# The passage from the output projection to the up projection in a decoder layer: weights in places of their own, operands made within the last output block, and a written order

## The chip, the cores and the metric

The kernel is one program on one core of a Trainium2 chip. A core has a matrix engine (TensorE, PE in the profile; its weight loads are listed apart as PEld), VectorE (DVE), ScalarE (ACT), GpSimd (POOL) and SyncE (SP), on whose queue this kernel issues all its DMAs. Each engine works through its own instructions in order and waits on semaphores for the others. The metric is the time of one execution in microseconds on the device.

## The reference

One layer on x of 2048 x 1024, in float32. The mixer's three head groups yield y, which is projected and added; then comes a gated, convolved feed-forward network with 2816 channels a half. What lies around the change:

```python
y = jnp.concatenate([y_attn, y_mlstm, y_sgu], axis=-1)
x = x + gt1 * (y @ w_out)                        # output projection
h = rms_norm(x, g_ffn) * (1.0 + sc2) + sh2       # 2048 x 1024
z = h @ w_up                                     # up projection, to 2 x 2816
z = causal_depthwise_conv(z, w_conv, b_conv)     # width 3
a, gv = jnp.split(z, 2, axis=-1)
x = x + gt2 * ((silu(a) * gv) @ w_down)
```

## The kernel before

**Precision.** A float32 operand is split into a high and a low half in fp32r, and a product is three matmuls: high by high, high by low, low by high (`mm3`, lines 54 to 56). Making the halves costs a cast on ScalarE (the high half) and a subtraction of two SBUF operands on another engine (the low half), mostly VectorE.

**The output projection** works on four blocks of 512 positions, `TBS = (2, 3, 0, 1)`. A block has eight parts (i, nb), 128 positions by 512 columns; a part is 24 matmuls of 128x512 into a bank of PSUM (`wps`), with operands `yhl0`/`yhl1` (the split y, loaded on SP as `yt_d` and, for half of them, `y2_d`, which are added on VectorE) and `wo0`/`wo1` (the split w_out). Loads pass through three buffers `ld`. A part is evicted on VectorE (`evict`: times gate, plus x, then squares on ScalarE). When both halves of a row tile are done, `stats` works out the scale of the norm (its last operation on GpSimd) and `scale` applies it on VectorE. When all four row tiles of a block are scaled, `turns` transposes them: eight tiles k, each of four 128x128 transposes on TensorE into a bank `tps` (four banks), then a copy on ScalarE to `hT[k]`, which is called hz in the trace. `turns` of a block stands within the parts of the next one, behind its part 1. Blocks 0 and 1 (positions 1024 to 2047, H = 1) are also made into operands of the up projection by `put_d` and written to memory as `hc_d` for later.

**The up projection** uses a product scheme with seven instead of eight block products. A group g is 128 columns of each half of w_up; H is the half of the positions. Its seven steps p = 1, 2, 5, 6, 7, 4, 3 take the operands B11, B21, T1, T2, T3, T4, B22, four tiles each of 512 columns, made once for each H from hT. B11 and B21 need only the first 512 positions of a half, thus the third output block; T1 = B12 - B11, T3 = B22 - B12, T2 = B22 - T1, T4 = B21 - T2 and B22 need the last one. The weights' side of a step is a quarter of the group's tiles w1, w2 or a combination of them, S1 or S2; `Group.prep` makes it and splits it (the tiles wsph and wspl), three steps ahead. `Group.mm` issues 12 matmuls, `Group.post` combines the results, and `conv` and `gate` follow as VectorE and ScalarE have time. The first two groups of H = 0 run interleaved: steps 0 and 1 are both groups' p = 1, steps 2 and 3 both groups' p = 2, then p = 5, and so on to step 13. Group 2 begins at step 14.

**What sets the order.** The instructions are written in an order by Python code, and a scheduler then reorders them on each engine by its own costs. In this kernel it interleaved the passage: one T1 matmul stands ahead of the steps on B21, and the combinations T1, T3, T2 and T4 alternate with S1, S2 on VectorE. Memory on the core is given out by pools that open and close like a stack on a left and a right side; a tile waits until the former user of its place is done. The weights `w` of the first two groups lie where `wo0` was, B11 where `yhl1` was, so both are made only when the output projection ends. `w_first`, the loads of these weights, are written behind the last output block.

The names and lines that matter: `load_split` (loads at 296 and 299, the addition at 300, casts at 130, low half at 131), `put` (1141 to 1154), `evict` (1182, rows L1186 and L1187), `stats` (1192), `scale` (L1200), `turn` (transposes L1208, copy L1209), `turns` (1213), `b_first`, `prep` (S1 and S2 at L1317 and L1318, casts L1327, low halves L1328), the step loop at the end, and `conv` (L1382, L1383, L1387).

Of the kernel before, what the change touches and what calls it, by code (L numbers as in the profile page):

```python
# [8 lines left out]
F32 = mybir.dt.float32  # L9
# [3 lines left out]
ALU = mybir.AluOpType  # L13
# [4 lines left out]
P = 128  # L18
# [15 lines left out]
def trunk(  # L34
# [278 lines left out]
    def up_open_right():  # L313
        pool.open("up_r1", "right", *[("act%d" % n, 4096, 1) for n in range(14, 22)], ("wsp", 2048, 12))
        pool.open("up_r2", "right", ("w", 4096, 4), ("B11", 4096, 4), ("B21", 4096, 4), ("T2", 4096, 4))

# [803 lines left out]

    pool.open("zy", "left", ("zy", 4104, 8))
    pool.open("wo_l", "left", ("hl", 4096, 4), ("gt1", 4096, 1), ("yg", 2048, 2), ("x2", 4096, 6), ("wst_", 8, 8))
# [17 lines left out]

    def put(n, q, t, by_dram=False):

        if n == "T2":
            src = t[:, 1, :].bitcast(F32) if by_dram else pool.tile([P, 512], F32, name="t2")
            V.tensor_tensor(src, h_part("B22", q), h_part("T1", q), op=ALU.subtract)
            V.tensor_tensor(h_part("T4", q), h_part("B21", q), src, op=ALU.subtract)
        else:
            src = h_part(n, q)
            if n == "T1":
                V.tensor_tensor(src, h_part("B12", q), h_part("B11", q), op=ALU.subtract)  # L1150
            elif n == "T3":
                V.tensor_tensor(src, h_part("B22", q), h_part("B12", q), op=ALU.subtract)
        A.copy(t[:, 0, :], src)
        V.tensor_tensor(t[:, 1, :], src, t[:, 0, :].bitcast(F32), op=ALU.subtract)

    def put_d(n, q):
        t = pool.tile([P, 2, 512], F32R, name="hl", tag="hl")
        put(n, q, t, True)
        dma(hc_d[COMBO.index(n), q], t.bitcast(F32))

    class Block:
# [50 lines left out]

        def turns(self):
            if self.half == 0:
                for k in range(KT):
                    self.turn(k)
                if self.H == 1:
                    for q in range(4):
                        todo.append(lambda q=q: (put_d("B11", q), put_d("B21", q)))
            else:  # L1220
                for q in range(4):
                    self.turn(q)
                    self.turn(4 + q)
                    if self.H == 1:
                        todo.append(lambda q=q: (put_d("T1", q), put_d("T3", q)))
                        todo.append(lambda q=q: (put_d("T2", q), put_d("T4", q), put_d("B22", q)))
# [4 lines left out]
    for n, tb in enumerate(TBS):  # L1231
# [3 lines left out]
        for j, (i, nb) in enumerate(parts):  # L1235
# [5 lines left out]
            if prev:  # L1241
                prev[0].evict(*prev[1:])
                if prev[2] == 1:
                    prev[0].stats(prev[1])
                    prev[0].scale(prev[1])
            if j == 1 and before:
                before.turns()
            if todo and j >= 1:
# [5 lines left out]
    while todo:  # L1254
        todo.pop(0)()
    pool.close("wo_r2")
    pool.close("wo_r")
    pool.close("att_s")
    pp.close("wo_r")
    up_open_right()  # L1260
    w_first = [w_load(0), w_load(1)]
    hb = {}

    def b_first(n, qs=range(4)):
        for q in qs:
            t = b_tile(n, q)
            hb.setdefault((0, n), []).append(t)
            put(n, q, t)

    blk.evict(0, 1)  # L1270
    b_first("B11", (0, 1))
    blk.stats(0)
    blk.scale(0)
    blk.evict(1, 1)
    b_first("B11", (2, 3))
    blk.stats(1)
    blk.scale(1)

# [9 lines left out]
    def up_open_left():  # L1288
        pool.open(
            "up_l", "left", ("s", 2048, 4), ("sw", 2048, 4), ("T1", 4096, 4), ("B22", 4096, 4), ("t2", 2048, 1), ("hal", 352, 1)  # L1290
        )
        pp.open("up_l", "left", ("ub1", 2048, 4))
# [4 lines left out]
    class Group:  # L1297
# [12 lines left out]
        def prep(self, p):  # L1310
# [4 lines left out]
            if p in (5, 6) and self.S1 is None:  # L1315
                self.S1, self.S2 = self.tmp("S1", "sw"), self.tmp("S2", "sw")
                V.tensor_tensor(self.S1, A_[2, 1], A_[2, 2], op=ALU.add)  # L1317
                V.tensor_tensor(self.S2, self.S1, A_[1, 1], op=ALU.subtract)  # L1318
            if p == 7:
# [30 lines left out]
        def post(self, p):  # L1350
            g, H = self.g, self.H
            if p == 1:
                self.s1 = self.tmp("s1", "s")
                A.copy(self.s1, self.X)
# [258 lines left out]
    for i in range(AHEAD):  # L1613
        up_groups(-1)
    prep(0)
    blk.evict(2, 1)
    blk.stats(2)
    prep(1)
    blk.scale(2, True)
    blk.evict(3, 1)  # L1620
    b_first("B21", (0, 1))
    blk.stats(3)
    b_first("B21", (2,))
    blk.scale(3, True)
    b_first("B21", (3,))
    prep(2)
    loaded = n_open + 1
    for i, s in enumerate(steps):
# [15 lines left out]
        if i == 1:  # L1644
            blk.turns()
            pool.close("wo_l")
            pp.close("wo_l")
            up_open_left()
            hal = pool.tile([P, 44, 2], F32, name="hal")
            V.memset(hal, 0.0)  # L1650
        if i >= n_open:
            while loaded < min(i + AHEAD + 3, n_left + AHEAD + 3 if i < n_left else len(steps)):
                load(loaded)
                loaded += 1
# [7 lines left out]
        if i:  # L1662
            q = steps[i - 1]
            if q[0] == "up":
                if q[1:] in ((0, 0, 2), (0, 1, 2)):
# [49 lines left out]
```

## Time and profile before

| | us |
|---|---|
| median of 3 runs | 2640.88 (2638.76 to 2641.74) |
| the profiled execution | 2639.6 |
| its span, first to last instruction | 2637.8 |
| mean granted TensorE clock | 0.994 of full speed |
| output projection, about | 1160 to 1349 |
| passage, about | 1349 to 1391 |
| up projection of the first groups | from 1391 |

The profile is of one execution. A row of the timeline gives the start, the duration, the engine, the line, the operation, the tiles it writes and reads, and in square brackets how long the engine was idle before it and what ended the wait. A window's row gives each engine's busy time in a stretch. Where engines are busy in the large stages can be seen in these windows (length; busy us and instructions of PE, PEld, DVE, ACT, POOL; granted clock; DMA share; GB/s), the second one from the passage on:

```text
1160.00:1350.00 190.00, 186.07 (x869) 153.00 (x868) 111.68 (x193) 74.25 (x150) 14.88 (x19) 1.00 0.66 228
1350.00:1440.00 90.00, 80.96 (x342) 64.98 (x341) 85.12 (x130) 54.51 (x100) 0.84 (x1) 0.94 0.28 85
1440.00:2000.00 560.00, 558.81 (x2465) 462.35 (x2464) 471.61 (x622) 268.98 (x449) 0.00 (x0) 1.00 0.33 110
```

### The profile page before, as it was taken

The page shows a single profiled execution, that of the slowest core. Times are in us where ns is not written, and L with a number is a line of the kernel's source. Part 1 is how long each engine was busy: PE and PEld are TensorE (multiplying, and loading weights), DVE is VectorE, ACT ScalarE, POOL GpSimd, SP SyncE. Part 2 cuts the span into 40 slices and gives each one's busy share as a digit, 9 for nine tenths or more (in the row PEclk, how much of TensorE's full clock was granted, in tenths as well). Part 3 has the DMA queues.
Part 4 walks back from the last instruction along what each step waited for, and adds up shares of the span by engine and source line. Part 5 has one row for each costly group of instructions (what it writes and reads, how often), then busy time and mean ns, then how long its engine had stood idle before and what let it go on. Part 6 is the DMA issues. An engine that isn't in the chain of part 4 may idle for free.

```text
span 2637.8 us, 36872 instructions
## 1 busy us (share of the span) xinstructions
PE 2559.2 (97%) x12761; PEld 2116.1 (80%) x12761; DVE 1994.9 (76%) x3454; ACT 1269.7 (48%) x2420; POOL 398.4 (15%) x530
## 2 busy tenths in 40 slices
PE   5999999999999999999989999999999999999999
PEld 4887888878787878777868888888888888888787
DVE  7477644565468888966769888887888888898797
ACT  4333334333367888853455454444444444444443
POOL 2012210122335665630000000000000000000000
PEclk9999999999999999999999999999999999999999
DMA  7554553324563345346723222236222226648523
GB/s 250 183 162 132 178 161 109 105 80 116 160 188 109 113 136 146 87 148 238 276 80 101 83 88 80 86 141 237 88 85 84 80 72 248 235 164 299 182 98 116
DMA packets 297986, 377.51 MB, mean 143 GB/s; under 512 B 31422, under 2 KB 189980, under 8 KB 295752
## 3 DMA queue, kind: packets, MB, share of 16 engines
q1 hardware_dynamic: 297800, 375.16, 44.4%
q8 instruction: 101, 1.65, 0.2%
q14 instruction: 85, 0.70, 0.1%
HBM read 274.34 MB, written 100.74 MB: 142 GB/s over the span
## 4 chain that ended last, share of the span: by engine, by line
PE 78%; DVE 9%; DMA 6%; issue 3%; ACT 2%; POOL 1%; SPq 1%; DVEq 0%; ACTq 0%; POOLq 0%
PE ub L56 10%; PE ub L55 10%; PE ub L54 10%; PE acc L54 6%; PE acc L56 6%; PE acc L55 6%; PE db L55 4%; PE db L56 4%; PE db L54 4%; PE sp L205 3%; PE tp L258 3%; PE op L244 2%; PE op L245 2%; DVE wspl L1459 1%; DMA wa<-in_w_ada_dram 1%
## 5 line engine op out<-in xcount | busy, mean ns | idle before, releaser
L54 PE MATMUL acc<-wh,hh 128*128 128x512 f32 (+2 forms) x768 | 287.6, 376 | 3.3 <-DVE ev L684 1.4
L54 PE MATMUL ub<-T,wsph 128*128 128x512 f32 x704 | 274.4, 390 | 5.8 <-ACT wsph L1327 5.8
L56 PE MATMUL acc<-wh,hl 128*128 128x512 f32 (+2 forms) x768 | 274.9, 361 | 1.9 <-DVE hl L562 1.9
L55 PE MATMUL acc<-wl,hh 128*128 128x512 f32 (+2 forms) x768 | 274.5, 359 | 0.0
L56 PE MATMUL ub<-T,wspl 128*128 128x512 f32 x704 | 273.9, 390 | 0.3 <-DVE wspl L1328 0.3
L55 PE MATMUL ub<-T,wsph 128*128 128x512 f32 x704 | 274.1, 389 | 0.0
L55 PE MATMUL db<-wspl,wsph 128*128 128x512 f32 x616 | 240.6, 391 | 2.8 <-DVE wspl L1459 2.7
L56 PE MATMUL db<-wsph,wspl 128*128 128x512 f32 x616 | 239.8, 390 | 0.0
L54 PE MATMUL db<-wsph 128*128 128x512 f32 x616 | 238.4, 390 | 0.3 <-ACT wsph L1458 0.3
L1327 ACT CAST wsph<-S 128x512 fp32r<-128x512 f32 x176 | 109.6, 623 | 228.7 <-PE ub L55 161.0
L262 DVE TENSOR_TENSOR plo<-tp,phi 128x512 fp32r<-128x512 f32 (+1 forms) x320 | 187.0, 607 | 31.5 <-ACT phi L261 29.2
L54 PE MATMUL ub<-B,wsph 128*128 128x512 f32 x528 | 207.4, 393 | 2.8 <-ACT wsph L1327 2.8
L56 PE MATMUL ub<-B,wspl 128*128 128x512 f32 x528 | 207.3, 393 | 0.8 <-DVE wspl L1328 0.8
L55 PE MATMUL ub<-B,wsph 128*128 128x512 f32 x528 | 207.3, 393 | 0.0
L222 ACT ACTIVATE L<-L,nm 128x1024 f32<-128x1024 f32 (+2 forms) x192 | 172.5, 902 | 36.4 <-DVE nm L211 35.1
L258 PE MATMUL tp<-ident,L 128*128 128x128 f32 x1088 | 177.1, 275 | 2.8 <-DVE plo L262 0.8
L261 ACT CAST phi<-tp 128x512 fp32r<-128x512 f32 (+1 forms) x320 | 159.8, 520 | 40.1 <-PE tp L258 38.8
L205 PE MATMUL sp<-kk,q 128*128 128x512 f32 (+3 forms) x640 | 169.4, 376 | 3.2 <-DVE nm L211 2.2
L227 POOL TENSOR_SCALAR L<-L,rs 128x1024 f32<-128x1024 f32 (+2 forms) x192 | 167.2, 881 | 11.0
L1458 ACT CAST wsph<-act 128x512 fp32r<-128x512 f32 x132 | 82.2, 623 | 179.1 <-PE db L55 162.7
L54 PEld LDWEIGHTS acc<-wh,hh 128*128 128x128 f32 x768 | 146.9, 192 | 23.1 <-DVE ev L684 1.6
L56 PEld LDWEIGHTS acc<-wh,hl 128*128 128x128 f32 x768 | 145.4, 190 | 24.2 <-DVE hl L562 2.7
(337 smaller groups left out, 5998.4 us busy)
## 6 DMA issues: line engine op xcount, KB each, us to landing
w<-in_w_up_dram SPq DMA_DIRECT2D x88, 512.0 KB
wd<-in_w_down_dram SPq DMA_DIRECT2D x176, 256.0 KB
wa<-in_w_ada_dram SPq DMA_DIRECT2D x96, 256.0 KB
act_d<-yc SPq DMA_DIRECT2D x44, 512.0 KB
act<-act_d SPq DMA_DIRECT2D x44, 512.0 KB
wr<-in_w_in_dram SPq DMA_DIRECT2D x64, 256.0 KB
q<-q_d SPq DMA_DIRECT2D x128, 128.0 KB
hc_d<-hl SPq DMA_DIRECT2D x28, 512.0 KB
```

The source lines that it names most:

```text
L54: T.matmul(ps, lh, rh, start=start, stop=False, skip_group_check=resume)
L55: T.matmul(ps, lh, rl, start=False, stop=False, skip_group_check=resume)
L56: T.matmul(ps, ll, rh, start=False, stop=stop, skip_group_check=resume)
L205: T.matmul(sp[:, b : b + bw], q2[n][:, qs], kk[:, s0 + b : s0 + b + bw], start=n == 0, stop=n == 1 and not last)
L222: A.activation(L[c], L[c], AF.Exp, bias=nm[:, n - 1 : n], scale=-1.0, accum_out=rs[:, c : c + 1])
L227: G.tensor_scalar(t, t, rs[:, 0:1], 1.0, op0=ALU.mult, op1=ALU.mult)
L244: T.matmul(op[:, c0:], vv[:, j, :], hi[:, c0:], start=(j == 0), stop=False)
L258: T.transpose(tp[:, i * P : (i + 1) * P], rows[i][j // 8][:, (j % 8) * P : (j % 8 + 1) * P], ident)
L261: A.copy(hi[:, c0:], tp[:, c0:])
L262: V.tensor_tensor(lo[:, c0:], tp[:, c0:], hi[:, c0:].bitcast(F32), op=ALU.subtract)
L1327: A.copy(hi, src)
L1458: A.copy(hi, v)
```

## The change

It has five parts. (1) The weights of the first two groups get places of their own: the tag `w` moves into the pool `zy` on the left, opened with the output projection; B11 and B21 move to where `wo0` and `yhl1` were, and s1 of the first two groups gets a tag `s0` of its own. The loads are written at part 0 of the last output block. (2) `turns` is split into two parts of four tiles, behind part 1 and part 2 of the next block. (3) B11 and the weights' halves of steps 0 and 1 are made ahead of the last four evictions, B21 between them. (4) From there to step 16, TensorE, VectorE and ScalarE run in the written order; the scheduler goes on for the others. Within it, `b_first` makes all four tiles of a combination before their halves, T1 and T2 first, and the transposes stand behind steps 0 and 1, with those steps' results copied out ahead. (5) S1 and S2 of the first two groups are worked out on GpSimd.

```diff
@@ pools
-        pool.open("up_r2", "right", ("w", 4096, 4), ("B11", 4096, 4), ("B21", 4096, 4), ("T2", 4096, 4))
+        pool.open("up_r2", "right", ("B11", 4096, 4), ("B21", 4096, 4), ("T2", 4096, 4), ("s0", 2048, 2))
...
-    pool.open("zy", "left", ("zy", 4104, 8))
+    pool.open("zy", "left", ("zy", 4104, 8), ("w", 4096, 4))
@@ put, now in pieces
+    def combine(n, q, src=None):
 
         if n == "T2":
             V.tensor_tensor(src, h_part("B22", q), h_part("T1", q), op=ALU.subtract)
+            return src
+        src = h_part(n, q)
+        if n == "T1":
+            V.tensor_tensor(src, h_part("B12", q), h_part("B11", q), op=ALU.subtract)
+        elif n == "T3":
+            V.tensor_tensor(src, h_part("B22", q), h_part("B12", q), op=ALU.subtract)
+        return src
+
+    def combine_t4(q, t2):
+        V.tensor_tensor(h_part("T4", q), h_part("B21", q), t2, op=ALU.subtract)
+
+    def halves_of(src, t):
         A.copy(t[:, 0, :], src)
         V.tensor_tensor(t[:, 1, :], src, t[:, 0, :].bitcast(F32), op=ALU.subtract)
@@ Block.turns and the loop over output blocks
+        def turns(self, part):
+            for q in range(4):
+                self.turn(4 * part + q)
+            if self.H == 1 and part == 1:
...
-            if j == 1 and before:
-                before.turns()
+            if j in (1, 2) and before:
+                before.turns(j - 1)
+            if (n, j) == (3, 0):
+                w_first = [w_load(0), w_load(1)]
@@ passage
+    in_order = tc.manual_schedule(engines={mybir.EngineType.PE, mybir.EngineType.DVE, mybir.EngineType.Activation})
+    in_order.__enter__()
...
-    w_first = [w_load(0), w_load(1)]
...
     def b_first(n, qs=range(4)):
+
+        if n == "T1":
+            for q in qs:
+                combine("T1", q)
+            for q in qs:
+                t2.append(combine("T2", q, pool.tile([P, 512], F32, name="t2", tag="s")))
+        elif n == "T3":
+            for q in qs:
+                combine("T3", q)
         for q in qs:
             t = b_tile(n, q)
             hb.setdefault((0, n), []).append(t)
-            put(n, q, t)
+            halves_of(t2[q] if n == "T2" else h_part(n, q), t)
+        if n == "T2":
+            for q in qs:
+                combine_t4(q, t2[q])
@@ Group.prep
-                V.tensor_tensor(self.S1, A_[2, 1], A_[2, 2], op=ALU.add)
-                V.tensor_tensor(self.S2, self.S1, A_[1, 1], op=ALU.subtract)
+                eng = G if self.H == 0 and self.g < 2 else V
+                eng.tensor_tensor(self.S1, A_[2, 1], A_[2, 2], op=ALU.add)
+                eng.tensor_tensor(self.S2, self.S1, A_[1, 1], op=ALU.subtract)
@@ last evictions and the step loop
+    b_first("B11")
     prep(0)
-    blk.evict(2, 1)
-    blk.stats(2)
     prep(1)
-    blk.scale(2, True)
-    blk.evict(3, 1)
-    b_first("B21", (0, 1))
...
+    for i in range(4):
+        blk.evict(i, 1)
+        blk.stats(i)
+        blk.scale(i, i > 1)
+        if i < 2:
+            b_first("B21", (2 * i, 2 * i + 1))
     prep(2)
...
         if i == 1:
-            blk.turns()
+            for q in steps[:2]:
+                groups[q[1], q[2]].post(q[3])
+            blk.turns(0)
+            blk.turns(1)
...
+        if i == 16:
+            in_order.__exit__(None, None, None)
```

What this makes of the instructions' order is seen at three places. The first is TensorE behind the last transposes of the passage. Before, one matmul on T1 stands there, ahead of the two steps on B21:

```order
L1208 MATMUL tps_14993<-ident_74,x2_14893 128x128
L1208 MATMUL tps_14993<-ident_74,x2_14912 128x128
L54 MATMUL ub_15108<-T1_15016,wsph_15036 128x512
L54 MATMUL ub_14925<-B21_14900,wsph_14917 128x512
L55 MATMUL ub_14925<-B21_14900,wsph_14917 128x512
```

In the changed kernel, on the same engine, the B21 steps follow at once:

```order
L1219 MATMUL tps_15000<-ident_74,x2_14908 128x128
L1219 MATMUL tps_15000<-ident_74,x2_14918 128x128
L54 MATMUL ub_14928<-B21_14879,wsph_14920 128x512
L55 MATMUL ub_14928<-B21_14879,wsph_14920 128x512
L56 MATMUL ub_14928<-B21_14879,wspl_14921 128x512
```

The first matmul on T1 has moved behind both B21 steps, 24 matmuls later. The second place is SP's queue at the loads of block 1's operands (`ld` from `yt_d` and `y2_d`; `x2_d` is the write of an evicted row tile), before:

```order
L296 DMA ld_13579<-yt_d_68 128x512
L299 DMA ld_13581<-y2_d_69 128x512
L296 DMA ld_13588<-yt_d_68 128x512
L299 DMA ld_13590<-y2_d_69 128x512
L296 DMA ld_13597<-yt_d_68 128x512
L1190 DMA x2_d_70<-x2_13276 128x1024
L299 DMA ld_13599<-y2_d_69 128x512
```

And the same stretch in the changed kernel, where `w1` and `w2` are the weights of the first two groups:

```order
L296 DMA ld_13580<-yt_d_68 128x512
L340 DMA w1_14557<-in_w_up_dram 128x8x128
L299 DMA ld_13582<-y2_d_69 128x512
L296 DMA ld_13589<-yt_d_68 128x512
L341 DMA w2_14558<-in_w_up_dram 128x8x128
L340 DMA w1_14561<-in_w_up_dram 128x8x128
L299 DMA ld_13591<-y2_d_69 128x512
L1201 DMA x2_d_70<-x2_13277 128x1024
L296 DMA ld_13598<-yt_d_68 128x512
L341 DMA w2_14562<-in_w_up_dram 128x8x128
L299 DMA ld_13600<-y2_d_69 128x512
```

Though written at the last block, the four loads stand two blocks earlier in the queue; the scheduler put them there. The third place is VectorE ahead of the last four evictions in the changed kernel, where before only evictions and scalings stood:

```order
L1158 TENSOR_TENSOR B11_14856<-hz_14611,B11_14856 128x512
L1158 TENSOR_TENSOR B11_14859<-hz_14618,B11_14859 128x512
L1345 TENSOR_TENSOR wspl_14863<-w1_14557,wsph_14862 128x512
L1345 TENSOR_TENSOR wspl_14867<-w1_14561,wsph_14866 128x512
L1197 TENSOR_TENSOR yg_14870<-wps_14717,gt1_13215 128x512
```

The low halves of B11 and of the weights of steps 0 and 1 are done there before the first of those evictions reads its bank.

More of the change, by code (lines that the diff above doesn't have):

```diff
@@ L1139, in h_part, with put @@
         return hT[i + q][:, j * 512 : (j + 1) * 512]
-    def put(n, q, t, by_dram=False):
+    def combine(n, q, src=None):
         if n == "T2":
-            src = t[:, 1, :].bitcast(F32) if by_dram else pool.tile([P, 512], F32, name="t2")
             V.tensor_tensor(src, h_part("B22", q), h_part("T1", q), op=ALU.subtract)
[L1146 to L1152, printed above, removed]
+            return src
[8 more added lines that the diff above has]
+    def halves_of(src, t):
         A.copy(t[:, 0, :], src)
         V.tensor_tensor(t[:, 1, :], src, t[:, 0, :].bitcast(F32), op=ALU.subtract)
+    def put(n, q, t):
+        src = combine(n, q, t[:, 1, :].bitcast(F32))
+        if n == "T2":
+            combine_t4(q, src)
+        halves_of(src, t)
     def put_d(n, q):
         t = pool.tile([P, 2, 512], F32R, name="hl", tag="hl")
-        put(n, q, t, True)
+        put(n, q, t)
         dma(hc_d[COMBO.index(n), q], t.bitcast(F32))
@@ L1211, in turn @@
             )
[L1213 to L1218, printed above, removed]
-                        todo.append(lambda q=q: (put_d("B11", q), put_d("B21", q)))
[L1220 to L1224, printed above, removed]
+        def turns(self, part):
+            for q in range(4):
+                self.turn(4 * part + q)
+            if self.H == 1 and part == 1:
+                for q in range(4):
+                    if self.half == 0:
+                        todo.append(lambda q=q: (put_d("B11", q), put_d("B21", q)))
+                    else:
                         todo.append(lambda q=q: (put_d("T1", q), put_d("T3", q)))
@@ L1260, in trunk @@
     up_open_right()
-    w_first = [w_load(0), w_load(1)]
     hb = {}
+    t2 = []
     def b_first(n, qs=range(4)):
+        if n == "T1":
[6 more added lines that the diff above has]
+                combine("T3", q)
         for q in qs:
@@ L1267, in b_first @@
             hb.setdefault((0, n), []).append(t)
-            put(n, q, t)
[L1270 to L1277, printed above, removed]
+            halves_of(t2[q] if n == "T2" else h_part(n, q), t)
+        if n == "T2":
+            for q in qs:
+                combine_t4(q, t2[q])
     pp.open("up_r", "right", ("ub0", 2048, 4))
@@ L1289, in up_open_left @@
         pool.open(
-            "up_l", "left", ("s", 2048, 4), ("sw", 2048, 4), ("T1", 4096, 4), ("B22", 4096, 4), ("t2", 2048, 1), ("hal", 352, 1)
+            "up_l", "left", ("s", 2048, 4), ("sw", 2048, 4), ("T1", 4096, 4), ("B22", 4096, 4), ("hal", 352, 1)
         )
@@ L1352, in post @@
             if p == 1:
-                self.s1 = self.tmp("s1", "s")
+                self.s1 = self.tmp("s1", "s0" if H == 0 and g < 2 else "s")
                 A.copy(self.s1, self.X)
@@ L1614, in trunk @@
         up_groups(-1)
+    b_first("B11")
     prep(0)
-    blk.evict(2, 1)
-    blk.stats(2)
     prep(1)
-    blk.scale(2, True)
-    blk.evict(3, 1)
-    b_first("B21", (0, 1))
[L1622 to L1625, printed above, removed]
+    for i in range(4):
[4 more added lines that the diff above has]
+            b_first("B21", (2 * i, 2 * i + 1))
     prep(2)
@@ L1663, in trunk @@
             q = steps[i - 1]
-            if q[0] == "up":
+            if i <= 2:
+                pass
+            elif q[0] == "up":
                 if q[1:] in ((0, 0, 2), (0, 1, 2)):
```

## The prediction

> **What bounds the kernel now.** I read the page first: its head, its busy row and the first row of its chain that ended last.
> ```profile
> span 2637.8 us, 36872 instructions
> PE 2559.2 (97%) x12761; PEld 2116.1 (80%) x12761; DVE 1994.9 (76%) x3454; ACT 1269.7 (48%) x2420; POOL 398.4 (15%) x530
> PE 78%; DVE 9%; DMA 6%; issue 3%; ACT 2%; POOL 1%; SPq 1%; DVEq 0%; ACTq 0%; POOLq 0%
> ```
> TensorE is busy for 97% of the span and carries 78% of the chain. No matmul is removed, so a gain can only come from TensorE's gaps and from stretches at a lower clock. The windows around the two edited places show where these are; after the length stand the busy times of PE, PEld, DVE, ACT and POOL, the granted clock, the DMA share and GB/s.
> ```profile
> 1200.00:1210.00 10.00, 8.78 (x38) 6.56 (x37) 7.56 (x15) 4.25 (x9) 1.10 (x2) 1.00 0.70 222
> 1210.00:1220.00 10.00, 8.19 (x51) 6.73 (x49) 5.78 (x9) 4.65 (x9) 0.00 (x0) 1.00 0.46 136
> 1350.00:1360.00 10.00, 6.44 (x22) 4.67 (x21) 8.41 (x16) 5.73 (x12) 0.84 (x1) 0.83 0.71 190
> 1360.00:1370.00 10.00, 4.83 (x28) 3.34 (x26) 7.35 (x13) 8.37 (x14) 0.00 (x0) 0.94 0.00 1
> 1370.00:1380.00 10.00, 10.00 (x33) 7.85 (x34) 10.00 (x18) 9.34 (x21) 0.00 (x0) 0.72 0.01 2
> 1380.00:1440.00 60.00, 59.69 (x264) 49.11 (x263) 59.36 (x85) 31.08 (x56) 0.00 (x0) 1.00 0.31 95
> ```
> From 1350 to 1370 TensorE works 11.27 of 20 us, and in the 10 us behind that it has a clock of 0.72. From 1380 on TensorE is full again, **but VectorE is full too** (59.36 of 60). That second fact decides this case. TensorE's own rows of the passage:
> ```profile
> 1326.36 0.39 PE L54 MATMUL wps<-wo0h,yhl0h 128*128 128x512 f32 x1
> 1348.58 0.39 PE L56 MATMUL wps<-wo1h,yhl0l 128*128 128x512 f32 x1
> 1353.09 0.50 PE L54 MATMUL ub<-B,wsph 128*128 128x512 f32 x1 [2.81 <-ACT wsph L1327]
> 1354.57 0.51 PE L56 MATMUL ub<-B,wspl 128*128 128x512 f32 x1 [0.75 <-DVE wspl L1328]
> 1362.46 2.66 PE L1208 MATMUL tps<-ident,x 128*128 128x128 f32 x16 [0.54 <-ACT hz L1209]
> 1369.72 0.80 PE L54 MATMUL ub<-T,wsph 128*128 128x512 f32 x1 [4.60 <-ACT wsph L1327]
> 1390.11 0.51 PE L56 MATMUL ub<-T,wspl 128*128 128x512 f32 x1 [0.31 <-DVE wspl L1328]
> 1427.65 0.39 PE L54 MATMUL ub<-T,wsph 128*128 128x512 f32 x1
> ```
> The first two rows are 98 matmuls apart: (1348.58 - 1326.36) / 98 = 0.2267 us each at full clock, so a step of 12 is 2.72 us. The last row is the first matmul of the T2 step of up group 3. Behind 1390.11 no wait stands up to it, and as both kernels issue the same matmuls in the same order from there on, its time measures what the passage gains or loses.
>
> **The passage.** By the changed order TensorE issues steps 0 and 1 (24 matmuls on B11) straight behind the last output matmul, at 1348.81 to 1348.81 + 24 x 0.2267 = 1354.25, since their operands are made ahead of the last four evictions; the 2.81 and 0.75 go. Next come the 32 transposes, for which the last row tile has to be scaled. VectorE's rows:
> ```profile
> 1343.56 0.69 DVE L1186 TENSOR_TENSOR yg<-wps,gt 128x512 f32<-128x512 f32 x1 [0.54 <-PE wps L56]
> 1346.93 0.76 DVE L1200 TENSOR_SCALAR x<-x,st 128x1024 f32<-128x1024 f32 x1 [0.75 <-POOL st L127]
> 1349.01 0.69 DVE L1186 TENSOR_TENSOR yg<-wps,gt 128x512 f32<-128x512 f32 x1 [1.32 <-PE wps L56]
> 1362.44 0.69 DVE L1150 TENSOR_TENSOR hz<-hz 128x512 f32<-128x512 f32 x1 [3.60 <-ACT hz L1209]
> 1368.29 2.50 DVE L1154 TENSOR_TENSOR T<-hz,T 128x512 fp32r<-128x512 f32 x4
> ```
> From eviction to the end of the scaling it is 1346.93 + 0.76 - 1343.56 = 4.13 us. The last eviction can start no earlier than now, 1349.01, so the tile is ready at 1353.14, ahead of 1354.25: the two steps hide that chain whole. The transposes then feed the eight ACT copies to hz:
> ```profile
> 1361.33 0.60 PE L1208 MATMUL tps<-ident,x 128*128 128x128 f32 x4
> 1361.63 5.46 ACT L1209 ACTIVATE hz<-tps,sh,a 128x512 f32<-128x512 f32 x8 [5.91 <-PE tps L1208]
> ```
> Their pitch is (5.46 - 0.78) / 7 = 0.67 us, 0.78 being my estimate of one alone. The first of them starts 0.3 us behind the last transpose of its tile (1361.33 to 1361.63), and a transpose is 2.66 / 16 = 0.17, so the first hz ends near 1354.25 + 3 x 0.17 + 0.3 + 0.78 = 1355.9 and the last near 1360.6. The B21 steps, now ahead of all T1 matmuls, run to about 1364.0, and the 4.60 goes. What would be late next on TensorE alone is nothing: 1348.81 + 22 steps x 2.72 + about 4.2 for the transposes puts the milestone near 1412.9, which is 14.8 earlier. Of that, 2.81 + 0.75 + 0.54 + 4.60 + 0.31 = 9.0 is waits and the other 5.8 matmuls at the reduced clock.
>
> **But VectorE is late next.** Its T1 work starts at 1362.44 now, and 1369.72's matmul waited for what hangs on it. In the changed order the chain from the first T1 combination to the low half of group 2's T1 weights is 68 operations on 128x512 and 3 on 128x1024. The pitch is (2.50 - 0.69) / 3 = 0.60 us, giving 68 x 0.60 = 40.8. For the 3 and their partner on ScalarE:
> ```profile
> L1383 DVE SCALAR_TENSOR_TENSOR yc<-zg,colC,yc 128x1024 f32<-128x1024 f32 x6 | 7.7, 1289 | 1.4 <-ACT yc L1382 1.4
> L1382 ACT ACTIVATE yc<-zg,colC 128x1024 f32<-128x1024 f32 x7 | 8.7, 1246 | 2.0 <-DVE zg L1368 2.0
> ```
> Three are 3 x 1.19 = 3.6 (1.29 less the 0.10 by which neighbours overlap). Written order adds waits that the earlier interleaving covered: five low halves stand right behind the in-place S1 or S2 they split, and wait for ScalarE's cast between (5 x 0.6 = 3.0), and two conv products wait for L1382, up to 1.25 each (2.3 together). Behind each of these, everything of VectorE is queued. The chain is 40.8 + 3.6 + 3.0 + 2.3 = 49.7 us.
>
> Its start: not before the first hz, 1355.9. The four S1/S2 operations of groups 0 and 1, now on GpSimd, run there too, from about 1352.4 (1349.01 + 4.13 less the scaling). GpSimd's nearest rows are these:
> ```profile
> L131 POOL TENSOR_TENSOR wo1l<-ld,wo1h x4: 1297/1539/1731, 1161.5 to 1181.0; 128x512 fp32r<-128x512 f32 x4
> L131 DVE TENSOR_TENSOR wo1l<-ld,wo1h x4: 679/1267/1796, 1162.0 to 1182.0; 128x512 fp32r<-128x512 f32 x4
> ```
> The same operation takes 1.30 to 1.73 on GpSimd, and on VectorE 0.68 alone but up to 1.80 while GpSimd runs. Four are at least 5.2, and if VectorE gives way throughout, 1359.5 is where it gets free. I take 1357.5, between the two. Then the low half is there at 1357.5 + 49.7 = 1407.2; ten matmuls and five steps later, 2.27 + 13.6, the milestone comes at 1423.1: **4.5 gained** of 14.8; bounds 2.5 (1359.5) and 6.1 (1355.9), and 11 if all waits for ScalarE (5.3) are covered as well. Behind that VectorE has some 16 us of work in a group's seven steps of 19.05 us, so nothing more is lost. Moving S1 and S2 saves VectorE 4 x 0.60 = 2.4, which is in the count of 68.
>
> The Trainium skill ("SBUF — State Buffer", section "SBUF: two separate sides") says that VectorE and GpSimd share a port pair as an exclusive lock: a VectorE operation with two SBUF inputs and a GpSimd operation that reads SBUF exclude each other, the loser fully blocked. The 1.27 beside 0.68 agrees, and by this rule the start is 1359.5 and the gain 2.5.
>
> **The split turns.** TensorE's rows in the output blocks before:
> ```profile
> 1206.97 0.50 PE L54 MATMUL wps<-wo0h,yhl0h 128*128 128x512 f32 x1 [1.22 <-ACT yhl0h L130]
> 1217.94 0.66 PE L1208 MATMUL tps<-ident,x 128*128 128x128 f32 x4 [1.80 <-ACT hz L1209]
> 1266.14 0.65 PE L1208 MATMUL tps<-ident,x 128*128 128x128 f32 x4 [0.69 <-ACT hz L1209]
> ```
> The transposes behind the first sixteen waited for a PSUM bank, 1.80 and 0.69. Now 24 output matmuls, 5.44 us, stand there, in which ScalarE copies four banks out (4 x 0.67 = 2.7). Both waits go: **2.5 gained**. If ScalarE's queue were held by casts of operands for 3 us more, it would be nothing, which is the lower bound. The last block's put_d work and hc_d writes keep their places within a part; I cost them nothing, as the loads of block 3's operands, for which TensorE waits longer, hide them.
>
> **The weights loaded early.** Four loads of 512 KB move from the passage up among block 1's operand loads, on the same SP queue. What a transfer of that size does to a load behind it:
> ```profile
> 1186.60 0.32 SPq L299 DMA_DIRECT2D ld<-y_d  x1
> 1194.32 0.32 SPq L1190 DMA_DIRECT2D x_d<-x  x1
> 1195.18 0.32 SPq L299 DMA_DIRECT2D ld<-y_d  x1
> 1189.58 0.69 DVE L300 TENSOR_TENSOR ld<-ld 128x512 f32<-128x512 f32 x1 [1.03 <-DMA ld<-y_d]
> 1199.88 0.69 DVE L300 TENSOR_TENSOR ld<-ld 128x512 f32<-128x512 f32 x1 [1.34 <-DMA ld<-y_d]
> ```
> Issue to use is 1189.58 - 1186.60 = 2.98, and 1199.88 - 1195.18 = 4.70 behind the 512 KB write: 1.7 dearer. Four make 6.8 us. TensorE is still in block 0's matmuls there and only waits at the end, the 1.22 above; I take one load and a part of the next, about 2.4 late against some 1.3 of cover, **1.1 lost**, between 0 and 4 (two loads in full plus what follows).
>
> **The sum** is 4.5 + 2.5 - 1.1 = 5.9. The profiled run took 2639.6 (its span 2637.8 and 1.8 around it); it becomes 2633.7. The median of the three runs is 2640.88, 1.3 above it, so I state 2635.0.
>
> **Rivals.**
> R1, VectorE isn't the bound, or only softly. For it: before, it is full without making TensorE wait behind 1390. Against: it would start only 5 us earlier than now. Without delay by GpSimd, 6.1 + 2.5 - 0 gives 2632.3; with ScalarE's waits covered, 11 + 2.5 - 1.1 gives 2628.5; with TensorE the bound, 2624.7.
> R2, given back: VectorE yields to GpSimd throughout (2.5) and the loads cost up to 4. That gives 2637.0 to 2639.9; the wo1l rows speak for it, and against it that some of GpSimd's operations fall in VectorE's waits for hz. The lock quoted above is this case.
> R3, slower: the loads delay the serial chain of block 1's operands, 12 loads over three buffers. At 1.3 each that is 15.6, less the 7.0 gained: 2649.5. It comes out slower from 12.3 lost, about ten loads of the twelve; the DMA share of 0.70 and the waits for DMA of only 1.03 and 1.34 speak against it.
> That the change doesn't do what it says is hardly open, the order of TensorE shows it; a wait in the old place, for T1's cast instead of B21, is contained in R2.
>
> **How the numbers follow.** Forecast (2632 to 2638) 0.52, R1 0.22, R2 0.20, R3 0.06. 0.2% is 5.3 us, about what a measurement tells from no change, so faster is below 2635.6. That holds for R1 and 0.32 of the forecast: 0.54. The forecast's rest and R2 are the 0.40 within it, R3 the 0.06. The range, 2630.0 to 2640.0, leaves out R3 and about half of R1.
>
> **What would show it.** No wait ahead of the first ub matmul; no 4.60; between 1360 and 1410 TensorE's waits name VectorE's wspl or ScalarE's wsph, 0.6 to 2 us each, while the granted clock stays near 1.00; the milestone near 1423. S1 and S2 on GpSimd at 1.3 us or more, with VectorE operations of over 1 us beside them. No waits at the second sixteen transposes; a longer wait than 1.22 at yhl0h in block 1, near 2.3. The forecast is wrong if VectorE shows idle time in 1360 to 1410 with TensorE full, or if the wait for yhl0h exceeds 4.

## The result, and the profile after

The changed kernel takes 2658.96 us (median of six runs, 2656.46 to 2663.2) against 2640.84 us before (six runs on the same chip). The ratio is 1.0072, with a 95% interval of 1.0062 to 1.0083: **slower by 0.7%**, where 2635.0 with a range of 2630 to 2640 was forecast. The profiled run took 2656.7 us, its span is 2654.6. The page's head, busy row and chain after:

```profile
span 2654.6 us, 36889 instructions
PE 2561.2 (96%) x12761; PEld 2118.8 (80%) x12761; DVE 1997.2 (75%) x3450; ACT 1269.7 (48%) x2420; POOL 405.5 (15%) x534
PE 76%; DVE 11%; DMA 6%; ACT 3%; issue 2%; POOL 1%; SPq 1%; DVEq 0%; ACTq 0%; POOLq 0%
```

TensorE's work is the same; its share of the chain fell from 78% to 76%, and VectorE's and ScalarE's rose by two and one. The same windows as before (length; busy us and instructions of PE, PEld, DVE, ACT, POOL; granted clock; DMA share; GB/s):

```profile
1200.00:1210.00 10.00, 7.79 (x24) 5.07 (x24) 6.49 (x14) 3.85 (x9) 1.10 (x2) 0.83 0.72 222
1350.00:1360.00 10.00, 7.38 (x21) 5.60 (x22) 6.25 (x13) 3.35 (x9) 0.75 (x2) 0.67 0.21 83
1360.00:1370.00 10.00, 1.77 (x7) 0.84 (x5) 5.92 (x12) 2.43 (x7) 1.05 (x3) 0.68 0.26 104
1370.00:1380.00 10.00, 7.77 (x39) 7.39 (x40) 9.57 (x10) 8.16 (x13) 6.51 (x5) 0.64 0.06 23
1380.00:1440.00 60.00, 50.58 (x211) 40.42 (x210) 53.47 (x79) 30.96 (x59) 0.00 (x0) 0.94 0.18 53
```

TensorE works 16.9 of the 30 us from 1350 to 1380, before 21.3, and nine more us are missing from 1380 to 1440. In 1360 to 1370 VectorE and ScalarE are idle for much of the time as well: nobody has much to do, so a chain of dependent steps holds all. TensorE's rows show where:

```profile
1351.84 0.76 PE L54 MATMUL ub<-B,wsph 128*128 128x512 f32 x1 [3.93 <-DVE yg L1197]
1357.85 0.47 PE L54 MATMUL ub<-B,wsph 128*128 128x512 f32 x1 [0.79 <-DVE yg L1197]
1361.98 0.33 PE L1219 MATMUL tps<-ident,x 128*128 128x128 f32 x1 [1.01 <-DVE x L1211]
1367.21 0.47 PE L1219 MATMUL tps<-ident,x 128*128 128x128 f32 x1 [4.90 <-DVE x L1211]
1372.23 5.77 PE L1219 MATMUL tps<-ident,x 128*128 128x128 f32 x29 [4.55 <-DVE x L1211]
1384.49 0.50 PE L56 MATMUL ub<-T,wspl 128*128 128x512 f32 x1 [0.57 <-DVE wspl L1345]
1403.75 0.76 PE L54 MATMUL ub<-T,wsph 128*128 128x512 f32 x1 [7.93 <-DVE u L1374]
1444.82 0.39 PE L54 MATMUL ub<-T,wsph 128*128 128x512 f32 x1
```

The old waits (2.81, 0.75, 0.54, 4.60) are gone, but the new ones are longer: for evictions (yg, whose reading frees a PSUM bank), for one scaled row tile after another (x), and for u. The last row is the prediction's milestone, the first matmul of group 3's T2 step: 1444.82 instead of 1427.65. **What the evictions wait for stands on ScalarE and VectorE:**

```profile
1347.26 0.62 ACT L1157 CAST B<-hz 128x512 fp32r<-128x512 f32 x1 [18.19 <-PE wps L56]
```

```profile
1347.91 1.97 DVE L1158 TENSOR_TENSOR B<-hz,B 128x512 fp32r<-128x512 f32 x3 [18.12 <-ACT B L1157]
1351.01 0.68 DVE L1197 TENSOR_TENSOR yg<-wps,gt 128x512 f32<-128x512 f32 x1
1357.03 0.68 DVE L1197 TENSOR_TENSOR yg<-wps,gt 128x512 f32<-128x512 f32 x1
1363.04 0.68 DVE L1197 TENSOR_TENSOR yg<-wps,gt 128x512 f32<-128x512 f32 x1
1367.07 0.68 DVE L1197 TENSOR_TENSOR yg<-wps,gt 128x512 f32<-128x512 f32 x1
1375.56 3.47 DVE L1148 TENSOR_TENSOR hz<-hz 128x512 f32<-128x512 f32 x4
```

ScalarE's cast of the second B11 tile waits 18.19 us **for an output matmul** (wps, L56). VectorE's low half waits for the cast, and the first of the four evictions, whose output part is complete at 1331, stands behind it in the written order. So all four run in a row from 1351.01 to 1367.07, six, six and four us apart, when the matmuls they used to hide under are over. The first T1 combination (last row) starts at 1375.56, 28.0 us behind the last output matmul (1347.52), instead of 13.9 before (1362.44 less 1348.58).

Why a B11 tile waits for an output matmul is told by the places that the built program gives out (bytes of a partition; the right side's stack grows downwards):

```text
yhl1   108128 to 124512     free from the end of block 2 on
wo1    124512 to 157280     read by all output parts with nb = 1
B11    118752 to 135136     changed kernel; its second tile 131040 to 135136
```

Three of B11's four tiles lie on `wo1`. The part of it under the second tile belongs to the row blocks k = 5 and k = 6, last read by the matmul at 1346.84, which ends at 1347.23; the cast starts at 1347.26. The first tile (118752 to 122848) lies on `yhl1`, and its cast ran at 1328.47 without a wait. So B11 and B21 are not where the description of the change puts them: neither lies on `wo0`, and all of B21 (135136 to 151520) lies on `wo1`. In the kernel before, `yhl1` was the place of the weights `w` (106464 to 122848), and B11 (122848 to 139232) lay on `wo1` but for its lowest 1664 bytes. The change moved it by 4096 bytes only. Its casts waited for output matmuls before, too, but there the last eviction read its bank (1349.01) ahead of B11's low halves.

In sum the span grew by 16.8 us: the time up to block 0 is 2.3 shorter (ahead of what the change edits; in the profile before, the granted clock was 0.5 for 6.8 us near 45 and for 6.8 us near 236, and in the profile after it was not), the output projection, from block 0's first matmul to the last output matmul, 1.3 longer (201.0 after 199.7), the passage, from there to the milestone, 18.2 longer (97.3 after 79.1), the rest 0.4 shorter.

### The profile page after: what moved, and what is told of

Its sections match the earlier page's. It is cut to its first block, busy times and chain, and to the rows that moved or that the text cites. A ratio compares the mean times of both kernels' runs of the same rounds, so it can differ in the third digit from the quotient of the medians.

```text
span 2654.6 us, 36889 instructions
## 1 busy us (share of the span) xinstructions
PE 2561.2 (96%) x12761; PEld 2118.8 (80%) x12761; DVE 1997.2 (75%) x3450; ACT 1269.7 (48%) x2420; POOL 405.5 (15%) x534
## 4 chain that ended last, share of the span: by engine, by line
PE 76%; DVE 11%; DMA 6%; ACT 3%; issue 2%; POOL 1%; SPq 1%; DVEq 0%; ACTq 0%; POOLq 0%
PE ub L54 10%; PE ub L56 10%; PE ub L55 10%; PE acc L54 6%; PE acc L56 6%; PE acc L55 6%; PE db L55 4%; PE db L56 4%; PE db L54 4%; PE tp L258 3%; PE sp L205 3%; PE op L244 2%; PE op L245 2%; DVE wspl L1476 1%; DMA wa<-in_w_ada_dram 1%
## 5 line engine op out<-in xcount | busy, mean ns | idle before, releaser
L56 PE MATMUL acc<-wh,hl 128*128 128x512 f32 (+2 forms) x768 | 274.6, 361 | 1.1 <-DVE st L517 0.8
L56 PE MATMUL ub<-T,wspl 128*128 128x512 f32 x704 | 274.7, 390 | 0.9 <-DVE wspl L1345 0.9
L56 PE MATMUL db<-wsph,wspl 128*128 128x512 f32 x616 | 239.6, 389 | 0.0
L56 PE MATMUL ub<-B,wspl 128*128 128x512 f32 x528 | 206.2, 390 | 0.0
L56 PEld LDWEIGHTS acc<-wh,hl 128*128 128x128 f32 x768 | 145.2, 190 | 23.3 <-DVE hl L562 1.9
```

The lines of the kernel that those rows point to most:

```text
L56: T.matmul(ps, ll, rh, start=False, stop=stop, skip_group_check=resume)
```

## Experiments

Theory A: the loss is B11's place together with the written order. Its rivals: GpSimd's S1 and S2 hold up VectorE (B), the early loads cost the time (C, or W for the output projection alone), and the split of the turns costs it (T). For each run the table gives the ratio to the kernel before and three stretches of its profile, in us: output projection, last output matmul to first T1 combination, and the passage.

| run | ratio (95%) | output projection | to T1 | passage |
|---|---|---|---|---|
| before | 1 | 199.7 | 13.9 | 79.1 |
| before_again | one run | 200.0 | 13.9 | 79.1 |
| the change | 1.0072 (1.0062 to 1.0083) | 201.0 | 28.0 | 97.3 |
| after_again | one run | 203.6 | 28.1 | 97.3 |
| b11_free | 1.0047 (1.0032 to 1.0063) | 207.1 | 19.5 | 89.3 |
| both_free | 1.0070 (1.0047 to 1.0092) | 207.2 | 13.1 | 81.3 |
| no_written_order | 1.0025 (1.0014 to 1.0037) | 204.8 | 14.2 | 80.7 |
| s_on_vector | 1.0089 (1.0066 to 1.0113) | 204.3 | 25.1 | 97.8 |
| turns_whole | 1.010 (1.008 to 1.0121) | 204.5 | 28.0 | 97.3 |
| weights_later | 1.0075 (1.0055 to 1.0096) | 201.0 | 28.1 | 97.3 |
| evictions_first | 1.0026 (1.0013 to 1.0039) | 205.4 | 13.3 | 81.6 |
| all_mended | 0.9993 (0.9983 to 1.0003) | 200.3 | 8.8 | 74.7 |
| t_chain | 0.9982 (0.9972 to 0.9991) | 198.3 | 8.8 | 73.9 |

The passage repeats to 0.1 us between executions of one kernel (the first two and the next two rows), so its differences are large against that. The output projection took 201.0 and 203.6 in the two profiles of the changed kernel, and 201.0 to 207.2 in the seven profiles that have both the split turns and the early loads.

**b11_free.** Padding moves B11 down onto yhl1.

```diff
-        pool.open("up_r2", "right", ("B11", 4096, 4), ("B21", 4096, 4), ("T2", 4096, 4), ("s0", 2048, 2))
+        pool.open("up_r2", "right", ("B11", 4096, 4), ("pad", 4096, 3), ("B21", 4096, 4), ("T2", 4096, 4), ("s0", 2048, 2))
```

> The changed kernel with 12 KB of padding between B11 and B21, so that B11's four tiles lie on yhl1's place, which no output matmul of the last block reads, instead of on wo1's. Theory A (in the changed kernel B11's casts wait for the last output matmuls, 18.19 us, and the last four evictions stand behind them in the written order): B11's halves are made by about 1335, the first eviction no longer waits for them, but the first B21 tiles still lie on wo1 and hold evictions two to four until about 1347; the first T1 combination starts near 1366 to 1370 instead of 1375.6, and the time is 2650 to 2655 instead of 2659. Theory B (GpSimd's S1 and S2 hold up VectorE, and that is the loss): 2659, as in the changed kernel. Theory C (the early loads of weights cost the time): 2659.

Measured: 2653.3 us, as theory A has it. The first T1 combination comes 19.5 us behind the last output matmul instead of 28.0. The first eviction goes at once; now it is B21's first tile, still over wo1, that waits on ScalarE:

```profile
1356.57 1.14 ACT L1157 CAST B<-hz 128x512 fp32r<-128x512 f32 x2 [11.62 <-PE wps L56]
```

**both_free.** B21 gets the place of T4 (its first two tiles over wo0), T4 that of B21; B21's third and fourth tile are made behind the second and the last eviction.

```diff
-        tag = {"T3": "act%d" % (14 + k), "T4": "act%d" % (18 + k)}.get(n, n)
+        tag = {"T3": "act%d" % (14 + k), "B21": "act%d" % (21 - k)}.get(n, n)
...
-        if i < 2:
-            b_first("B21", (2 * i, 2 * i + 1))
+        if i != 2:
+            b_first("B21", ((0, 1), (2,), (), (3,))[i])
```

> As b11_free, and B21 too on a place that is free at the end of the first half of the last block (over wo0, with T4 in B21's former place); its third and fourth tile are made behind the second and the last eviction. Theory A: no cast of these operands waits for an output matmul, the four evictions follow the output parts as before the change, the first T1 combination starts at 1357 to 1361 and the time is 2638 to 2645. Theory B: T1 starts where it did, 2659. Theory C: 2659.

In the passage it did what theory A says: 13.1 us to T1, 81.3 for the passage, 16.0 less than in the changed kernel. Step 0 now follows the last output matmul (1357.06) at once, as the prediction had it:

```profile
1357.30 0.39 PE L54 MATMUL ub<-B,wsph 128*128 128x512 f32 x1
```

The time did not follow, 2658.5 us, which theory A had not foreseen. T4 is needed longer than B21, and at the end of the up projection, where the place is given to the down projection, a wait appears that the changed kernel doesn't have:

```profile
2223.14 0.79 PE L54 MATMUL db<-wsph 128*128 128x512 f32 x1 [7.81 <-ACT wsph L1475]
```

That swap costs 9.9 us there (up projection 794.6 us from the milestone on, 784.7 in the others), and this execution's output projection was 6 us longer. The ratio therefore says nothing on the passage; the profile does.

**no_written_order.** The changed kernel without the region in written order.

```diff
-    in_order = tc.manual_schedule(engines={mybir.EngineType.PE, mybir.EngineType.DVE, mybir.EngineType.Activation})
-    in_order.__enter__()
...
-        if i == 16:
-            in_order.__exit__(None, None, None)
```

> The changed kernel, its places of B11 and B21 included, without the written order: the scheduler orders TensorE, VectorE and ScalarE in the passage too, and puts the four evictions ahead of B11's halves. Theory A: the casts of B11 still wait for the last output matmuls, but nothing waits behind them, and the evictions are done by about 1353; time 2638 to 2648. Theory B: S1 and S2 still run on GpSimd, 2655 to 2659. Theory C: 2659.

2646.4 us and a passage of 80.7: theory A. B11 lies where it did and waits as it must, but the scheduler put the evictions ahead of it. The last one reads its bank right behind its output part (last matmul at 1352.54), and the low halves of B11 come behind it:

```profile
1352.97 0.69 DVE L1197 TENSOR_TENSOR yg<-wps,gt 128x512 f32<-128x512 f32 x1 [1.32 <-PE wps L56]
```

Neither the places nor the order alone makes the loss; both together do. The three runs also speak against theories B and C: S1 and S2 are still on GpSimd in them and the loads still early.

**s_on_vector.** `eng = V` for S1 and S2.

> The changed kernel with S1 and S2 of the first two groups back on VectorE. Theory A: the evictions are held as before, only the 1.0, 1.0 and 2.2 us by which VectorE's scaling, T1 combinations and weights' halves were longer beside GpSimd go, less 2.4 for the four operations: 2656 to 2659. Theory B: the loss goes, 2640 to 2645.

2664.2 us, not faster: B falls, and A's 2656 to 2659 was too low by 5 (the output projection in its profile is 3.3 us longer than in that of the changed kernel). T1 starts 3.0 us earlier, as no VectorE operation is lengthened, and the chain behind it is 3.5 longer (milestone less T1 72.8 instead of 69.3) with four more operations. Moving S1 and S2 is worth 0.5 us of the passage (97.3 instead of 97.8) where they run now.

**turns_whole and weights_later** take back one part each, at the output projection.

```diff
@@ turns_whole
-            if j in (1, 2) and before:
-                before.turns(j - 1)
+            if j == 1 and before:
+                before.turns(0)
+                before.turns(1)
@@ weights_later
-            if (n, j) == (3, 0):
-                w_first = [w_load(0), w_load(1)]
+            if (n, j) == (3, 3):
+                w_first = [w_load(g_, blk.x[3]) for g_ in (0, 1)]
...
+        if behind is not None:
+            for w in (w1, w2):
+                G.tensor_copy(w[:, 0, 0:1], behind[:, 0:1])
```

> The changed kernel with turns in one part again, all eight tiles behind part 1 as before the change. The stretch from the first matmul of block 0 to the last output matmul took 199.7 us before the change, and 201.0, 204.8 and 204.3 in the three profiles of the changed output projection. Theory T (the split leaves only sixteen transposes as work for TensorE ahead of the wait for the last operand of block 3, whose landing is set by the DMA queue): that wait falls from 2.2 to 4.4 us to 0 to 1.5, the waits for a bank, 1.8 and 0.7, come back, and the stretch is 200 to 203. Theory W (the early loads of weights delay the operands of blocks 1 and 3): the wait for block 3's operand stays at 2 to 4.5, and the stretch is 203 to 207. The passage behind it stays as it is in the changed kernel, 97.3 us from the last output matmul to group 3's T2 step; time 2656 to 2662.

> The changed kernel with the weights of the first two groups loaded later: their tiles are first touched by a one-column copy on GpSimd that needs the last x tile of block 3, so the four loads stand behind all loads of the output projection, when the DMA queues are idle. Theory W: the waits for operands fall to 1.2 in block 1 and to 0.2 in block 3, and the stretch to the last output matmul is 197 to 200 us instead of 201 to 205. Theory T: block 1's wait falls, block 3's stays at 2 or more, stretch 200 to 203. The passage stays at 97 us or gets longer, if the weights' halves come late. Time 2653 to 2659.

The decisive row is the first wait for block 3's last operand. In the changed kernel, in turns_whole and in weights_later:

```profile
1312.67 0.50 PE L54 MATMUL wps<-wo0h,yhl0h 128*128 128x512 f32 x1 [2.19 <-ACT yhl0h L130]
```

```profile
1318.14 0.50 PE L54 MATMUL wps<-wo0h,yhl0h 128*128 128x512 f32 x1 [0.18 <-ACT yhl0h L130]
```

```profile
1313.96 0.50 PE L54 MATMUL wps<-wo0h,yhl0h 128*128 128x512 f32 x1 [2.67 <-ACT yhl0h L130]
```

With the turns whole it is 0.18, with the weights later it stays at 2.67: theory T for this wait. All profiles of the table agree: 2.19 to 4.71 in the eight with the split turns, 0.20 or less in the five with whole ones. The transposes that moved behind part 2 had been the work that covered it. But turns_whole did not get shorter, 204.5 instead of the 200 to 203 of theory T, and its time, 2665.7, is above the 2656 to 2662 expected: in block 1 its waits are 2.63 for an operand and 1.89 for a bank, each followed by 3.4 us at half clock. So the early loads seem to cost something too: with the turns whole, the projection takes 204.5 with early loads, and 198.3 to 200.3 with late ones (the two profiles of the kernel before, all_mended and t_chain). How much the split and the loads are worth by themselves stays open, as the projection of like kernels differs by up to 6 us. The passage is 97.3 in both runs, so the loss there is due to neither.

**evictions_first.** B11 on yhl1 by the padding, and the order changed.

```diff
     for i in range(4):
         blk.evict(i, 1)
-        blk.stats(i)
-        blk.scale(i, i > 1)
-        if i < 2:
-            b_first("B21", (2 * i, 2 * i + 1))
+        if i:
+            blk.stats(i - 1)
+            blk.scale(i - 1, i > 2)
+    blk.stats(3)
+    blk.scale(3, True)
+    b_first("B21")
```

> The changed kernel with B11 on yhl1's place (12 KB of padding), and in the written order the four evictions ahead of B21's halves, each scaling behind the next eviction. Theory A: nothing that waits for an output matmul stands ahead of an eviction, so the last eviction follows its output part at once, as before the change, the first T1 combination starts 9 to 12 us behind the last output matmul instead of 28.0, and the passage takes 77 to 80 us instead of 97.3; time 2638 to 2646 with the output projection as changed. If VectorE's serial chain of eviction, squares, scale is what holds the passage, whatever the places: 88 us or more, 2650.

2647.8 us, 1.8 above the range expected; the passage falls from 97.3 to 81.6, so the serial chain by itself is not the hold. The last 1.6 us to what was expected are on VectorE beside GpSimd, which works on S1 and S2 from 1358.33 to 1364.68:

```profile
1356.63 0.75 DVE L1211 TENSOR_SCALAR x<-x,st 128x1024 f32<-128x1024 f32 x1 [0.76 <-POOL st L127]
1358.39 1.78 DVE L1211 TENSOR_SCALAR x<-x,st 128x1024 f32<-128x1024 f32 x1 [0.75 <-POOL st L127]
1360.10 5.73 DVE L1158 TENSOR_TENSOR B<-hz,B 128x512 fp32r<-128x512 f32 x4
```

The same scaling takes 0.75 and 1.78, four halves 5.73 instead of 2.50: 4.3 us, on the path to T1.

**all_mended.** Turns whole, evictions first, B11 on yhl1, the weights later and on the place of the hl tiles, which leaves room to make S1 and S2 ahead of the evictions, and the scheduler from step 2 on.

```diff
-    pool.open("zy", "left", ("zy", 4104, 8), ("w", 4096, 4))
+    pool.open("zy", "left", ("zy", 4104, 8), ("w", 4096, 4), ("sw", 2048, 4))
...
-        t = pool.tile([P, 2, 512], F32R, name="hl", tag="hl")
+        t = pool.tile([P, 2, 512], F32R, name="hl", tag="w")
...
+    for g_ in (0, 1):
+        groups[0, g_].s_pair()
     b_first("B11")
...
-        if i == 16:
+        if i == 2:
             in_order.__exit__(None, None, None)
```

> The mends together: turns whole, weights loaded later (on the place of the hl tiles), B11 on a free place, evictions first, S1 and S2 on GpSimd ahead of the evictions in a place of their own, and the written order only up to step 1, so that the scheduler orders the T chain as it did before the change. Expected from the parts: output projection 199 to 201 us as before, first T1 combination 9 to 11 us behind the last output matmul (before: 13.9), the chain from there 45 us as the scheduler's order took (written order: 51.9), so the passage is 69 to 74 instead of 79.1 before the change; time 2631 to 2636, faster than both kernels. If the passage is held by something else, 2640 or more.

The stretches came out close to what was expected: 200.3, 8.8 to T1 (9 to 11), 74.7 for the passage (69 to 74). The time, 2637.1, is 1 us above the range given; its interval reaches from 0.17% faster to 0.03% slower than before, so it isn't shown to be faster. VectorE's rows of T1, and TensorE's largest wait that is left:

```profile
1359.55 2.43 DVE L1151 TENSOR_TENSOR hz<-hz 128x512 f32<-128x512 f32 x4
```

```profile
1382.45 0.50 PE L54 MATMUL ub<-T,wsph 128*128 128x512 f32 x1 [2.54 <-ACT wsph L1354]
```

**before_again, after_again and t_chain.** The first two are the two kernels once more. t_chain is all_mended with two steps of the T chain in another place:

```diff
-        if n == "T2":
+        if n == "T3":
             for q in qs:
                 combine_t4(q, t2[q])
...
-            if p == 7:
+            two = self.H == 0 and self.g < 2
+            if p == (6 if two else 7):
                 V.tensor_tensor(self.S1, A_[1, 1], A_[2, 1], op=ALU.subtract)
```

> The kernel before the change once more, for its profile alone: how far its output projection (199.7 us from the first matmul of block 0 to the last output matmul) and its waits for operands (1.22 in block 1, 0.20 in block 3) differ between executions. If the changed kernels' longer stretches (201.0 to 207.2) are only such spread, 201 or more here; if the change causes them, 199 to 200.5.

> The changed kernel once more, for its profile alone. Theory A: the passage is 97.3 us again and B11's second cast waits some 18 us for the last output matmuls; the output projection lies anywhere from 201 to 205.

> all_mended, and in the T chain the difference T4 is formed behind the halves of T3 instead of ahead of T3's differences, and S1's second value is formed as soon as its first has been split. In all_mended TensorE still waits 2.54 and 2.03 us at the steps on T3 and has 6.8 us at half clock behind it. Expected: those waits fall to 0 to 2.5 together, the passage from 74.7 to 70 to 73 us, and the time by 2 to 4 us, to 2633 to 2636; unchanged at 2637 if VectorE's total work up to group 2 is the limit and not its order.

The kernel before stays at 200.0 us in its output projection, so the longer stretches come with the change. after_again repeats the passage (97.3). t_chain takes 2636.3 us against 2641.2 of the kernel before: 0.18% faster (0.09% to 0.28%), and so faster than both kernels. But its own edit did not do what was expected: the waits at the T3 steps are 4.68 and 0.96, together 1.1 more than in all_mended, and the passage is only 0.8 shorter. That it is clear of the kernel before, and all_mended not, isn't shown to come from this edit, as the two intervals overlap.

```profile
1380.62 0.80 PE L54 MATMUL ub<-T,wsph 128*128 128x512 f32 x1 [4.68 <-ACT wsph L1355]
```

## Why the prediction was wrong

**The step that failed** is the one on which the passage was built: steps 0 and 1 go "at 1348.81 to 1348.81 + 24 x 0.2267 = 1354.25, since their operands are made ahead of the last four evictions". They are written ahead of them, and the order shows them there; but they could not be made there. The prediction names no wait for their places, and so takes these as free by then; it never worked out which tiles they cover. With the operands late, the written order turned from what hides the chain of the last eviction into what holds up four of them. The experiments show both halves of this: with a free place 97.3 falls to 89.3 and 81.3, without the written order to 80.7.

This step is 16.0 of the 22.8 us by which the passage missed its forecast (97.3 instead of 1423.1 less 1348.6, 74.5). The other 6.8 are still there in both_free, where the step comes true: T1 starts 13.1 us behind the last output matmul and not 8.9, and from T1 to the milestone it takes 68.2 us and not 1423.1 less 1357.5, 65.6.

**"The last eviction can start no earlier than now, 1349.01"** held as a bound, but the eviction came at 1367.07. Where nothing blocks (all_mended), T1 starts 8.8 us behind the last output matmul; forecast was 1357.5 less 1348.6, 8.9. That the two agree is in part luck: 1.6 of the 8.9 was for GpSimd, which in all_mended is done with S1 and S2 at 1340.4.

**The chain on VectorE** was sized 2.2 us too short. Forecast were 49.7 us from the first T1 combination to the low half of group 2's T1 weights; after the change they are 51.9:

```profile
1426.74 0.68 DVE L1345 TENSOR_TENSOR wspl<-S,wsph 128x512 fp32r<-128x512 f32 x1
```

(1426.74 + 0.68 less 1375.56). The in-place waits are there, four of 0.74 to 0.76. With what follows it is 69.3 from T1 to the milestone, where the kernel before took 65.2 (1427.65 less 1362.44) with the scheduler's order. So the written order made this chain longer (68.2 to 69.8 in the runs that keep it with S1 and S2 on GpSimd, 65.1 to 66.5 in those that leave the chain to the scheduler): with T1 at 8.8 it would leave, by my estimate, 79.1 less 8.8 less 69.3, 1.0 us of gain. The 4.4 that all_mended got is beside the forecast 4.5 by luck, as its T chain is in the scheduler's order. That VectorE is late next, and not TensorE, holds: in all_mended VectorE is busy for all of 1370 to 1390, TensorE for 14.0 of these 20 us. That both kernels issue the same matmuls in the same order behind 1390.11 doesn't quite hold, as group 2 has its T1 step ahead of its B21 step in the changed kernel; the 22 steps ahead of the milestone are the same. The 7.93 us for u was not named: T3's products go into the bank that u's addition reads, and in the written order that addition stands behind the halves of T3 and T4. It is a wait within the same chain.

**GpSimd.** S1 and S2 took 1.26 to 1.72 us each, as the wo1l rows said, and VectorE's operations beside them were lengthened. The page "SBUF — State Buffer" of the Trainium skill, section "SBUF: two separate sides", says that the loser of the shared ports is blocked for the whole instruction; the trace agrees (in the changed kernel a scaling of 1.75 instead of 0.75, four T1 combinations of 3.47 instead of 2.49). By that rule GpSimd was to put off the start of T1 by 3.6 us (1359.5 less 1355.9), and 1.6 was taken; s_on_vector shows 3.0. It was weighed as a rival and is not the cause of the loss.

**The split turns** were to give 2.5 and took more than they gave. The waits for a bank did go, but the wait for block 3's operand grew from 0.20 to 2.19, and to 4.71 in other profiles: the prediction held that the loads of block 3's operands hide what moves there, and it is just there that work was missing.

**The early weights** were to cost 1.1, by a wait in block 1 of about 2.3. The wait is 2.09:

```profile
1205.06 0.50 PE L54 MATMUL wps<-wo0h,yhl0h 128*128 128x512 f32 x1 [2.09 <-ACT yhl0h L130]
```

By itself this shows little, as before_again has a wait of 1.95 there without these loads. Over all profiles the wait is 1.72 to 2.97, on average 2.4, in the eight with early loads and 0 to 1.95, on average 1.3, in the five without: about the 1.1 forecast. Half speed for 3.4 us follows it in all eight, and in three of the five others; a sum of waits leaves that out. Together with the split, the output projection lost 1.3 to 7.5 us in the seven profiles that have both, where a gain of 1.4 was forecast.

**The rivals.** The one that ended slower, the serial chain of block 1's operands, was not it: that chain cost a wait of 2 us. None of the rivals asked whether an instruction that was moved ahead can run there.

## What to carry to other kernels

An instruction that is moved ahead runs there only if everything it needs is there, and its own place in memory belongs to that: work out, tile by tile, who last read the bytes that it writes. Under a written order each such wait falls on all that stands behind it, so put what others wait for (evictions that free banks) ahead of what may be late. And ask of a wait that is removed by moving work what that work was covering where it stood.

## What the runs showed that was not expected

Half clock can follow a short wait of TensorE. In after_again and before_again a wait of 1.72 and of 1.95 us in block 1 was followed by a stretch of 3.41 us at a granted clock of 0.50, and in the changed kernel one of 2.09; in the first profile of the kernel before, waits of 1.22 and 1.80 were not. The length of the wait doesn't decide it alone: behind the 2.19 and 2.67 us in block 3 of the changed kernel and of weights_later the clock stayed at 1.00. The Trainium skill ("TensorE: Matmul & The Clock Gate", section "HAM oscillation — how this bites in real kernels") warns of idle gaps over some 3.4 us; here gaps of half that length were enough at times, and the measurement decides. Such a stretch costs, by my estimate, up to 1.7 us of matmul time (3.41 at half speed), about as much as the wait itself.
